# Modulation vectors on VectorE, GpSimd out of block 2's streams, a narrower product of the probabilities' remainder

## The chip, the cores and the metric

One core of a Trainium2 chip runs the whole program in one launch. The metric is the device time of that core in microseconds, from a launch with all inputs in the chip's memory to the output written; the number quoted is the median of several runs.

## The reference

Two transformer blocks, one after the other, of two layers each. The width is 1024; there are 256 latent tokens and 256 context tokens, and only the latent ones leave (so the second layer of each block computes no context output). Everything is float32.

```python
# block 1, layer l; the same for ctx with c_ctx while l == 0
m = split(silu(c) @ ada_w[l] + ada_b[l], 6)           # six modulation vectors of 1024
h = modulate(x, m[0], m[1])                           # x * (1 + scale) + shift
y = even_mixer(h, h_ctx) if l % 2 == 0 else odd_mixer(h, h_ctx)
x = layer_norm(alpha * x + m[2] * y)
x = layer_norm(alpha * x + m[5] * conv_ffn(modulate(x, m[3], m[4])))   # 1024 -> 2*2816 -> 1024
# block 2, layer l; the same for ctx while l == 0
m = split(silu(c) @ w_mod[l] + b_mod[l], 6)
h = rms_norm(x, g_pre_mix) * (1 + m[1]) + m[0]
y = token_mixer(h, hc)    # conformer conv + differential attention (8 heads) + multiscale pool, gated
x = x + m[2] * rms_norm(y, g_post_mix)
h = rms_norm(x, g_pre_ffn) * (1 + m[4]) + m[3]
x = x + m[5] * rms_norm(swiglu(h), g_post_ffn)                         # 1024 -> 2*2816 -> 1024
# differential attention, for each head
a = softmax(q1 k1) - lam * softmax(q2 k2);  o = a @ v
```

The six modulation vectors of a layer are a product of one row (latent) or two rows (latent and context) with a 1024 x 6144 matrix. There are four such matrices, one for each layer.

## The kernel before

**Products.** A float32 product is made of three products of rounded values: each operand is split into a rounded high part and a remainder, and `mm3` issues high x high, high x remainder and remainder x high. Weights come in 128-row pieces of up to 1024 columns: `wload` (L149) puts one into a tile `wr`, of which there are four, from the queue of SyncE; `wsplit` (L154) rounds it on ScalarE (`wh`, L159) and subtracts on VectorE or, if asked, on GpSimd (`wl`, L161). The tiles `wh` and `wl` have three buffers each.

**Order.** In the mixers (even, odd, and block 2's token mixer) the order is written out by hand: `main_stream` and a weaving function place lists of small steps (products of a group, attention units, extra items) one after the other. A `Stream` holds the weights of such a stage; splits from number `first` on go to GpSimd. In the FFNs the order of instructions on each engine is left to the framework's scheduler.

**Modulation vectors.** `ada` (L176) makes a list of items for a layer: eight chunks for each vector (128 rows of the matrix by 1024 columns), then a `bias` item (adds the bias, and for the two gates writes them to memory), and a `turn` item (transposes) for the others. A chunk runs in one of two ways. With no `acc_pool`, TensorE multiplies it: four unrounded matmuls, one for each quarter of the columns, on 32 of the array's columns each (L194). With `acc_pool` set (the large FFNs, of 512 tokens), VectorE multiplies the chunk by a column of silu(c) and adds it to a running sum (L201 for the first chunk, L204 for the others), once for the latent row and, where context is needed, once more; after the eighth chunk TensorE sums over the partitions with four matmuls for each of these rows (`pick`). A chunk occupies one `wr` tile until it is used.

Which items run where: the even mixer takes the rest of the first layer's vectors and as much of the second's as fits (eight items in each of five groups and 18 at the end, 58 in all); block 1's first FFN the remaining 38, on VectorE; the odd mixer 40 of block 2's first layer, in `extra` (14 and 22 at its end); block 1's second FFN (256 tokens, one item for each of its 22 pairs) the remaining 18, on TensorE; block 2's first FFN all 58 of block 2's second layer, on VectorE.

**A large FFN**: pairs of up-products j = 0 to 3 for each half of the tokens; pairs 4 to 10, with two items each; the first half of the down-product (two phases `nb`, six weight pieces each, one item after each piece); pairs 11 to 21, with two or three items each; the rest of the items; `mid()`, which prepares the next layer's factors; and the second half of the down-product.

**Block 2's attention** (`b2_attn`): for each head, the q, k, v products from a stream, rotary embedding (`rope`, L561, whose last addition is on GpSimd, L569), the stacking of q and k (L589), scores, softmax, the combination of the two probabilities on VectorE (L1516), transposes and the product with v. In that product the transposed probabilities H (rounded) and L (remainder) meet v, which lies as [high | remainder] in 256 columns; the result is later the sum of both halves of `oo`. Beside it the 31-tap convolution runs on VectorE (L1638).

**Gates of block 2's FFN.** `gg_bc` (L1315) loads the gain `g_post_ffn` into a tile `z`, the gate into `gbc`, and multiplies them on VectorE (L1322), at the FFN's start.

## Time and profile before

| | us |
|---|---|
| runs (three) | 2651.8, 2650.45, 2657.49 |
| median | 2651.8 |
| the profiled execution, as a run | 2655.9 |
| its span (first to last instruction) | 2654.1 |

The stages in the profiled span, by the lines that run: even mixer to 273, its output product and norm to 346, block 1's first FFN to 712, odd mixer to 842, its output to 895, block 1's second FFN to 1104, block 2's first attention stage to 1380, its branches and output product to 1703, its first FFN to 2082, the second attention stage to 2300, branches and output to 2456, and the last FFN to the end. The profile's page gives the busy time of each engine, PE being TensorE's matmuls, PEld its weight loads, DVE VectorE, ACT ScalarE, POOL GpSimd and SP SyncE; it also follows the chain of work that ended last. The granted clock is the clock that TensorE was given, as a share of full speed; its mean in this run is 0.983. A record's duration of a matmul is longer than its step, since matmuls overlap in the array: the distance from one start to the next is what a matmul takes in a sequence.

### The profile page before, as it was taken

What the parts mean: (1) busy time and instruction counts of PE and PEld (TensorE: products, weight loads), DVE (VectorE), ACT (ScalarE), POOL (GpSimd) and SP (SyncE); (2) the same over time, 40 slices, a digit from 0 to 9 for tenths busy, and PEclk for the clock granted to TensorE, in tenths of its full rate; (3) what the DMA queues carried; (4) which work ended last, traced back from release to release, by engine and by line L of the source; (5) the groups of instructions that cost most, each with busy time, mean ns of one, the idle gap of its engine ahead of it and who ended that gap; (6) DMA issues with size and microseconds to landing.
All of it is one profiled execution on the core that took longest, in us unless ns stands there. A gap on an engine that the chain in (4) does not pass through costs nothing.

```text
span 2654.1 us, 40807 instructions
## 1 busy us (share of the span) xinstructions
PE 2515.9 (95%) x15516; PEld 2183.4 (82%) x15516; DVE 1852.0 (70%) x3226; ACT 1230.0 (46%) x2329; POOL 407.9 (15%) x483
## 2 busy tenths in 40 slices
PE   7899899999998899999989999999999999898998
PEld 4787698788875799998877878888887999798997
DVE  5766797576877877556679755775457777887554
ACT  3554464144455555556652233532224565554543
POOL 4231100000121000243320000000000244200000
PEclk9999999999999899999999999999999999999999
DMA  8344766453556676531212234565656521356554
GB/s 270 112 153 162 265 213 194 157 166 108 178 178 218 197 232 188 175 88 54 66 53 88 88 96 150 177 199 177 192 163 195 158 80 61 95 161 208 171 182 147
DMA packets 129828, 412.37 MB, mean 155 GB/s; under 512 B 16640, under 2 KB 24992, under 8 KB 129632
## 3 DMA queue, kind: packets, MB, share of 16 engines
q1 hardware_dynamic: 119296, 386.45, 46.1%
q0 software_dynamic: 10048, 23.30, 2.9%
q8 instruction: 122, 2.00, 0.3%
q14 instruction: 74, 0.61, 0.1%
q10 hardware_dynamic: 288, 0.02, 0.0%
HBM read 408.59 MB, written 1.11 MB: 154 GB/s over the span
## 4 chain that ended last, share of the span: by engine, by line
PE 70%; DVE 13%; issue 6%; DMA 6%; ACT 4%; POOL 2%; SPq 0%; POOLq 0%; DVEq 0%; ACTq 0%
PE mm L168 62%; PE ax L168 3%; DVE wl L161 2%; DMA wr<-in_ada_w 2%; PE mm L194 1%; PE ax L600 1%; POOL rs_r L292 1%; DMA wr<-in_w_mod 1%; PE ax L611 1%; DVE ptl L615 1%; DMA gbc<-gd 1%; DMA s0w<-in_ada_w 1%; DVE cv L1638 1%; DVE p L1516 1%; ACT wh L159 1%
## 5 line engine op out<-in xcount | busy, mean ns | idle before, releaser
L159 ACT CAST wh<-wr 128x1024 fp32r<-128x1024 f32 (+2 forms) x580 | 572.4, 990 | 858.2 <-PE mm L168 669.1
L161 DVE TENSOR_TENSOR wl<-wr,wh 128x1024 fp32r<-128x1024 f32 (+2 forms) x494 | 570.5, 1158 | 273.1 <-ACT wh L159 270.4
L168 PE MATMUL mm<-hH,wh 128*128 128x256 f32 (+1 forms) x2176 | 708.5, 326 | 5.1 <-ACT wh L159 4.5
L168 PE MATMUL mm<-hH,wl 128*128 128x256 f32 (+1 forms) x2176 | 703.4, 324 | 3.5 <-DVE wl L161 3.3
L168 PE MATMUL mm<-hL,wh 128*128 128x256 f32 (+1 forms) x2176 | 703.2, 323 | 0.0
L168 PEld LDWEIGHTS mm<-hH,wh 128*128 128x128 f32 x2176 | 416.6, 192 | 46.6 <-issue 6.2
L168 PEld LDWEIGHTS mm<-hH,wl 128*128 128x128 f32 x2176 | 416.3, 191 | 37.0 <-DVE wl L161 5.3
L168 PEld LDWEIGHTS mm<-hL,wh 128*128 128x128 f32 x2176 | 416.6, 191 | 31.2
L168 PE MATMUL mm<-wh,hH 128*128 128x384 f32 (+1 forms) x864 | 278.2, 322 | 0.7 <-DVE hH L338 0.7
L168 PE MATMUL mm<-wl,hH 128*128 128x384 f32 (+1 forms) x864 | 270.4, 313 | 3.4 <-DVE wl L161 1.8
L168 PE MATMUL mm<-wh,hL 128*128 128x384 f32 (+1 forms) x864 | 269.7, 312 | 0.3 <-DVE hL L342 0.3
L161 POOL TENSOR_TENSOR wl<-wr,wh 128x768 fp32r<-128x768 f32 (+1 forms) x86 | 182.4, 2128 | 261.5 <-ACT wh L159 214.7
L168 PE MATMUL mm<-wh,gH 128*128 128x512 f32 x528 | 206.6, 392 | 3.4 <-DVE tm L1080 2.3
L168 PE MATMUL mm<-wl,gH 128*128 128x512 f32 x528 | 206.5, 391 | 2.8 <-DVE wl L161 2.8
L168 PE MATMUL mm<-wh,gL 128*128 128x512 f32 x528 | 206.0, 390 | 0.0
L168 PEld LDWEIGHTS mm<-wh,hH 128*128 128x128 f32 x864 | 164.9, 191 | 9.8 <-issue 6.9
L168 PEld LDWEIGHTS mm<-wl,hH 128*128 128x128 f32 x864 | 165.0, 191 | 6.9 <-DVE wl L161 2.7
L1638 DVE SCALAR_TENSOR_TENSOR cv<-u,cconv_w,cv 128x512 f32<-128x512 f32 (+1 forms) x240 | 168.4, 704 | 2.6
L168 PEld LDWEIGHTS mm<-wh,hL 128*128 128x128 f32 x864 | 164.7, 191 | 0.5 <-DVE hL L342 0.5
L204 DVE SCALAR_TENSOR_TENSOR adacc<-wr,cs,adacc 128x1024 f32<-128x1024 f32 x83 | 105.6, 1283 | 78.3 <-DMA wr<-in_w_mod 48.1
L292 POOL TENSOR_TENSOR rs_r<-rs_v,mhalf 128x1 f32<-128x1 f32 x44 | 41.6, 947 | 668.3 <-DVE rs_v L313 374.1
L168 PEld LDWEIGHTS mm<-wh,gH 128*128 128x128 f32 x528 | 99.4, 188 | 25.7 <-issue 4.8
(340 smaller groups left out, 4016.0 us busy)
## 6 DMA issues: line engine op xcount, KB each, us to landing
wr<-in_up SPq DMA_DIRECT2D x192, 512.0 KB, 3.8
wr<-in_dn SPq DMA_DIRECT2D x100, 512.0 KB, 3.8
wr<-in_w_mod SPq DMA_DIRECT2D x96, 512.0 KB, 4.4
wr<-in_ada_w SPq DMA_DIRECT2D x80, 512.0 KB, 4.6
wr<-in_wg SPq DMA_DIRECT2D x48, 512.0 KB, 3.5
wr<-in_glu SPq DMA_DIRECT2D x24, 512.0 KB, 3.8
wr<-in_qkv SPq DMA_DIRECT2D x32, 384.0 KB, 3.1
wr<-in_wo SPq DMA_DIRECT2D x24, 512.0 KB, 4.1
```

The costliest lines, as they stand in the source:

```text
L159: nc.scalar.copy(h[:, :n], w[:, :n])
L161: eng.tensor_tensor(l[:, :n], w[:, :n], h[:, :n], ALU.subtract)
L168: self.nc.tensor.matmul(o, s, m, start=start, stop=stop, skip_group_check=True)
L194: nc.tensor.matmul(st["pa"][32 * j:32 * j + 32, 0:256], a, x[:, j * 256:(j + 1) * 256], start=start, stop=stop, skip_group_check=True, til ...
L204: nc.vector.scalar_tensor_tensor(st["acc"][r], wt, cs[:, k, r:r + 1], st["acc"][r], ALU.mult, ALU.add)
L292: self.nc.gpsimd.tensor_tensor(o, i, self.mhalf[:, 0:n], ALU.pow)
L600: nc.tensor.transpose(pt[:, i * P:(i + 1) * P], s, self.idr)
L611: nc.tensor.transpose(pt[:, i * P:(i + 1) * P], s, self.idn)
L615: nc.vector.tensor_tensor(L, pt, H, ALU.subtract)
L1516: nc.vector.scalar_tensor_tensor(p0, p1, c[:, i:i + 1], p0, ALU.mult, ALU.add)
L1638: nc.vector.scalar_tensor_tensor(o, cb["u"][c][:, :, j:j + 256], cb["w"][:, c, j:j + 1], o, ALU.mult, ALU.add)
```

## The change

Three parts.

First, the items of `ada` are now kept by vector, and the vectors are dealt out anew. The even mixer gets vectors 2, 4 and 3 of its own layer alone (29 items: 5, 5, 5, 5, 4 in its groups and the rest at the end); block 1's first FFN gets vector 5 of that layer and 1, 0, 2, 4, 3 of the second layer (58 items, on VectorE); the odd mixer vectors 1, 0, 2 of block 2's first layer (29 items: 9 before its last group, the rest at the end); block 1's second FFN vector 5 of its own layer and 4, 3 of block 2's first (29 items, one for each of 14 pairs, then two); block 2's first FFN vector 5 of its own layer and all of the second's (67 items, on VectorE). Each chunk in a large FFN costs one or two units of credit, by its rows; each of the 30 places there adds 2.9 units, items run as long as the credit lasts, and a place stops after an item without a load. The gates' loads of block 1's FFNs are issued at the first use, `gg_bc` of block 2's FFNs in `mid()`.

Second, block 2's two streams no longer give splits to GpSimd, and its `rope` adds on VectorE. The powers of the norms stay on GpSimd, and so do the splits that the even and odd mixers give it.

Third, in block 2's product of probabilities and v, the remainder L is multiplied by v's high half only; L times v's remainder is left out.

```diff
-    def __init__(self, b, first=0, pool=None, n=0):
+    def __init__(self, b, first=None, pool=None, n=0):
...
-            self.hl[r] = self.b.wsplit(w, self.items[i][1], r >= self.first, own)
+            self.hl[r] = self.b.wsplit(w, self.items[i][1], self.first is not None and r >= self.first, own)
...
+    SHARE = 2.9
...
-                items.append((w[k * P:(k + 1) * P, m * D:(m + 1) * D], lambda wt, f=prod, k=k: f(wt, k=k)))
+                items.append((w[k * P:(k + 1) * P, m * D:(m + 1) * D], lambda wt, f=prod, k=k: f(wt, k=k),
+                              2 if parts.index(m) < ctx else 1))
                 if k == 1 and late is not None:
-                    items.append((None, late))
-            items.append((None, bias))
+                    items.append((None, late, 0))
+            items.append((None, bias, 0))
             late = None if m in (2, 5) else turn
-        if late is not None:
-            items.append((None, late))
-        return items
+            if m == 3:
+                items.append((None, late, 0))
+                late = None
+        return res
...
+    def share_ada(self, items, n):
+
+        self.credit += n
+        while items and items[0][2] <= self.credit:
+            self.credit -= items[0][2]
+            ap = items[0][0]
+            self.run_ada(items, 1)
+            if ap is None:
+                break
+        if not items:
+            self.credit = 0
...
-        nc.gpsimd.tensor_tensor(o, o, t2, ALU.add)
+        (eng or nc.gpsimd).tensor_tensor(o, o, t2, ALU.add)
...
-            gr["extra"] = self.stream_ada(ws, ada, (0, 8, 8, 8, 8, 8)[g])
+            gr["extra"] = self.stream_ada(ws, ada, (0, 5, 5, 5, 5, 4)[g])
...
-        last = self.stream_ada(ws, ada, 18)
+        last = self.stream_ada(ws, ada, 100)
...
-        extra = (0, 0, 4, 14, 22)
+        extra = (0, 0, 4, 9, 100)
...
                 for j in range(self.SKEW, 11):
                     up_pair(j, 0, 2)
-                    self.run_ada(ada, 2)
+                    self.share_ada(ada, self.SHARE)
                 for nb in range(2):
-                    banks = self.mmT(units(0, nb), gstat, range(4), 512, each=lambda: self.run_ada(ada, 1))
+                    banks = self.mmT(units(0, nb), gstat, range(4), 512, each=lambda: self.share_ada(ada, self.SHARE))
                     for t in range(4):
                         evac(t, nb, banks[t], 0)
                 for j in range(11, 22):
                     up_pair(j, 0, 2)
-                    self.run_ada(ada, 2 if j < 20 else 3)
+                    self.share_ada(ada, self.SHARE)
                 self.run_ada(ada, 100)
                 self.acc_pool = None
                 mid()
...
                 for j in range(NFF):
                     up_pair(j, 0, 1)
-                    self.run_ada(ada, 1)
+                    self.run_ada(ada, 1 if j < 14 else 2)
...
-            gts = {r: self.gate_bc(pool, key, 1, r, f"gbc{r}") for r in segs}
+            gts = {}
...
             def evac(t, nb, bank, kh):
+                if not gts:
+
+                    gts.update({r: self.gate_bc(pool, key, 1, r, f"gbc{r}") for r in segs})
...
-                            self.rope(pool, f, n64(b[:, 0:256]), rt("c", t, 4), rt("s", t, 4), 4)
+                            self.rope(pool, f, n64(b[:, 0:256]), rt("c", t, 4), rt("s", t, 4), 4, nc.vector)
...
                     self.mm(oo, H[:, c:c + P], vk, k == 0, False)
-                    self.mm(oo, L[:, c:c + P], vk, False, k == nk - 1)
+
+                    self.mm(oo[:, 0:P], L[:, c:c + P], vk[:, 0:P], False, k == nk - 1)
...
-            gg = self.gg_bc(pool, key, 1, segs, A["g_post_ffn"][l:l + 1])
+            gg = {}
...
             def mid():
+                gg.update(self.gg_bc(pool, key, 1, segs, A["g_post_ffn"][l:l + 1]))
...
-                    self.even_mixer(self.pool(s2, "att"), a0)
+                    self.even_mixer(self.pool(s2, "att"), a0[2] + a0[4] + a0[3])
...
-            self.b1_ffn(0, 512, a0, "b1l1")
+            self.b1_ffn(0, 512, a0[5] + a1[1] + a1[0] + a1[2] + a1[4] + a1[3], "b1l1")
...
-                    self.odd_mixer(self.pool(s2, "att1"), self.pool(s2, "att1u"), a2)
+                    self.odd_mixer(self.pool(s2, "att1"), self.pool(s2, "att1u"), a2[1] + a2[0] + a2[2])
...
-            ws = Stream(self, 10)
+            ws = Stream(self)
...
-            self.b1_ffn(1, 256, a2, None, early, late)
+            self.b1_ffn(1, 256, a1[5] + a2[4] + a2[3], None, early, late)
...
-            self.b2_ffn(0, 512, a3, False)
+            self.b2_ffn(0, 512, a2[5] + a3[1] + a3[0] + a3[2] + a3[4] + a3[3] + a3[5], False)
...
-            ws = Stream(self, 12)
+            ws = Stream(self)
```

## Rows read from the trace of the kernel before

**Rows 1.** The page: busy time by engine; shares of the last chain.
```profile
PE 2515.9 (95%) x15516; PEld 2183.4 (82%) x15516; DVE 1852.0 (70%) x3226; ACT 1230.0 (46%) x2329; POOL 407.9 (15%) x483
...
PE 70%; DVE 13%; issue 6%; DMA 6%; ACT 4%; POOL 2%; SPq 0%; POOLq 0%; DVEq 0%; ACTq 0%
```

**Rows 2.** Windows: stretch, length, busy PE, PEld, DVE, ACT, POOL, clock, DMA, GB/s.
```profile
65.00:273.00 208.00, 196.55 (x1452) 164.99 (x1451) 141.19 (x342) 109.79 (x301) 51.13 (x54) 0.99 0.46 149
457.00:521.00 64.00, 60.83 (x273) 49.18 (x272) 34.42 (x42) 14.57 (x17) 1.96 (x4) 1.00 0.49 158
712.00:842.00 130.00, 117.91 (x953) 90.15 (x952) 103.19 (x245) 66.93 (x158) 31.71 (x40) 0.95 0.56 177
1104.00:1380.00 276.00, 258.86 (x1705) 247.35 (x1703) 182.00 (x423) 163.96 (x442) 109.16 (x79) 0.99 0.25 75
...
2082.00:2300.00 218.00, 203.68 (x1633) 197.49 (x1632) 168.71 (x410) 130.37 (x318) 84.59 (x79) 0.98 0.27 82
...
895.00:1070.00 175.00, 174.69 (x1302) 160.25 (x1301) 132.92 (x209) 99.84 (x155) 5.21 (x10) 1.00 0.67 212
1800.00:1866.00 66.00, 66.00 (x305) 53.90 (x304) 34.78 (x38) 15.45 (x19) 1.96 (x4) 1.00 0.54 170
```

**Rows 3.** Timeline of PE around one chunk (start, duration, engine, line, operation).
```profile
196.18 0.28 PE L168 MATMUL mm<-ptl,v 128*128 128x256 f32 x1
196.39 0.64 PE L194 MATMUL mm<-wr,cs 128*32 128x256 f32 x8
...
197.24 0.34 PE L168 MATMUL mm<-wl,hH 128*128 128x384 f32 x1
```

**Rows 4.** Timeline of PE in block 2's product with v.
```profile
1256.71 0.28 PE L168 MATMUL ax<-v,pth 128*128 128x256 f32 x1
...
1256.83 0.28 PE L168 MATMUL ax<-v,ptl 128*128 128x256 f32 x1
```

**Rows 5.** Chain of waits at the odd mixer's end (start, duration, what).
```profile
817.33 5.47 DMA wr<-in_w_mod
...
826.52 7.88 DMA wr<-in_w_mod
```

**Rows 6.** Groups, whole span: xcount | busy us, mean ns | idle before.
```profile
L161 DVE TENSOR_TENSOR wl<-wr,wh 128x1024 fp32r<-128x1024 f32 x432 | 525.9, 1220 | 218.9 <-ACT wh L159 216.4
...
L204 DVE SCALAR_TENSOR_TENSOR adacc<-wr,cs,adacc 128x1024 f32<-128x1024 f32 x83 | 105.6, 1283 | 78.3 <-DMA wr<-in_w_mod 48.1 <-DMA wr<-in_ada_w 29.9
...
L194 PE MATMUL ax<-adacc,pick 128*32 128x256 f32 x88 | 6.6, 389 | 2.0 <-DVE adacc L204 2.0
```

**Rows 7.** Chain of waits at the start of block 2's first FFN.
```profile
1688.18 7.68 DMA z<-in_g_post_ffn
...
1695.96 1.22 DVE gbc L1322
```

**Rows 8.** POOL's subtractions in the first, then the second attention stage's window.
```profile
L161 POOL TENSOR_TENSOR wl<-wr,wh 128x768 fp32r<-128x768 f32 x32 | 60.7, 1907 | 80.9 <-ACT wh L159 78.4 <-PE mm L168 2.5
...
L161 POOL TENSOR_TENSOR wl<-wr,wh 128x1024 fp32r<-128x1024 f32 x24 | 58.8, 2452 | 75.9 <-ACT wh L159 63.1 <-issue 12.6
```

**Rows 9.** DVE: L1516 in the first, the second stage; L1638 there, over the span.
```profile
L1516 DVE SCALAR_TENSOR_TENSOR p<-p,cs,p 128x512 f32<-128x512 f32 x16 | 19.7, 1233 | 0.6
...
L1516 DVE SCALAR_TENSOR_TENSOR p<-p,cs,p 128x512 f32<-128x512 f32 x16 | 12.0, 752 | 0.6
...
L1638 DVE SCALAR_TENSOR_TENSOR cv<-u,cconv_w,cv 128x256 f32<-128x256 f32 x60 | 44.6, 743 | 0.4
...
L1638 DVE SCALAR_TENSOR_TENSOR cv<-u,cconv_w,cv 128x256 f32<-128x256 f32 x120 | 72.8, 612 | 0.7
```

**Rows 10.** Windows around two idle stretches of PE, columns as in rows 2.
```profile
1698.00:1704.00 6.00, 2.72 (x9) 2.13 (x10) 6.00 (x10) 3.46 (x6) 0.00 (x0) 0.66 0.07 6
...
2452.00:2458.00 6.00, 4.52 (x19) 3.77 (x19) 3.35 (x7) 2.33 (x6) 1.12 (x2) 0.50 0.58 188
2458.00:2464.00 6.00, 6.00 (x40) 5.99 (x40) 4.17 (x8) 2.04 (x4) 0.00 (x0) 0.74 0.07 29
```

More of the change, by code (lines that the diff above doesn't have):

```diff
@@ L188, in ada @@
         cs = self.cs[blk]
-        items, late = [], None
+        res, late = {}, None
         for m in parts:
-            st = {}
+            st, items = {}, []
+            res[m] = items
             def quarter(st, j, a, x, start, stop):
@@ L255, in run_ada @@
             if items:
-                ap, f = items.pop(0)
+                ap, f, _ = items.pop(0)
                 f(None if ap is None else self.wload(ap, D))
+    def share_ada(self, items, n):
[7 more added lines that the diff above has]
+        if not items:
+            self.credit = 0
     def stream_ada(self, ws, items, n):
@@ L263, in stream_ada @@
             if items:
-                ap, f = items.pop(0)
+                ap, f, _ = items.pop(0)
                 if ap is None:
@@ L558, in unit_slots, with rope @@
         return slots
-    def rope(self, pool, o, src, cosT, sinT, n):
+    def rope(self, pool, o, src, cosT, sinT, n, eng=None):
         nc = self.nc
@@ L1387, in e1 @@
                         if full:
-                            self.rope(pool, f, n64(b[:, 0:256]), rt("c", t, 4), rt("s", t, 4), 4)
+                            self.rope(pool, f, n64(b[:, 0:256]), rt("c", t, 4), rt("s", t, 4), 4, nc.vector)
                         else:
                             o = (h % 2) * P
-                            self.rope(pool, f[:, 0:2], n64(qs[t][:, o:o + P]), rt("c", t, 2), rt("s", t, 2), 2)
-                            self.rope(pool, f[:, 2:4], n64(b[:, 0:P]), rt("c", t, 2), rt("s", t, 2), 2)
+                            self.rope(pool, f[:, 0:2], n64(qs[t][:, o:o + P]), rt("c", t, 2), rt("s", t, 2), 2, nc.vector)
+                            self.rope(pool, f[:, 2:4], n64(b[:, 0:P]), rt("c", t, 2), rt("s", t, 2), 2, nc.vector)
                     else:
@@ L1655, in pool_items, with b2_mixer @@
         return [f for gi in range(4) for f in self.mmF_items(ws, self.A[f"wp{l}"][gi], lambda k: self.rhs(k, 0, T), T, done)]
-    def b2_mixer(self, l, T, cb, after, ws, pre, rate, ada=()):
+    def b2_mixer(self, l, T, cb, after, ws, pre, rate):
         nc, A = self.nc, self.A
@@ L1934, in build @@
             a3 = self.ada("b2l1", 2, A["w_mod"][1], A["b_mod"][1], ctx=2)
-            self.b2_mixer(0, 512, cb[0], lambda: after(0), ws, self.glu_items(ws, 0, cb[0], 0, 1), 1.0, a3)
-            self.b2_ffn(0, 512, a3, False)
+            self.b2_mixer(0, 512, cb[0], lambda: after(0), ws, self.glu_items(ws, 0, cb[0], 0, 1), 1.0)
+            self.b2_ffn(0, 512, a2[5] + a3[1] + a3[0] + a3[2] + a3[4] + a3[3] + a3[5], False)
             self.lst.close()
-            ws = Stream(self, 12)
+            ws = Stream(self)
             self.b2_mixer(1, 256, cb[1], lambda: after(1), ws, self.glu_items(ws, 1, cb[1], 0, 1), 0.6)
```

8 lines of the change are left out of this document (4 added, 4 removed).

## The prediction

> **What bounds the kernel now.** First the page's busy line and the chain of work that ended last [rows 1]: TensorE is busy for 95% of the span and 70% of that chain is TensorE; VectorE stands second with 70% busy and 13% of the chain, GpSimd has 15% and 2%. So work taken from TensorE counts nearly in full wherever TensorE is itself the limit, and VectorE is the engine to which this change adds. Next the same by stage, because the average hides where VectorE has room [rows 2]. TensorE is idle for 11.5 us of the 208 in the even mixer, 12.1 of 130 in the odd one, 0.3 of 175 in block 1's second FFN, 17.1 of 276 and 14.3 of 218 in the two attention stages of block 2. VectorE is at 79% in the odd mixer and 77% in the second attention stage, but only at 54% and 53% in the two stretches of the large FFNs where the product with the down weights runs. Last the rows of single instructions, for prices.
>
> **1. Modulation chunks leave the mixers.** One chunk (128 of the 1024 rows of one vector's weights) is eight records on TensorE. From the matmul before it to the second matmul after it the starts are 1.06 us apart [rows 3]; without it there would be one step of 256 columns, 0.12 [rows 4], and one of 384, 0.18 in proportion. So a chunk costs 0.76 us. The even mixer goes from 49 chunks to 24 (from 58 list items to 29): 25 x 0.76 = 19.0 us less. Against it stands what they cover: the list spread over its last units falls from 18 items to 5, and where TensorE would otherwise wait, a chunk was free. With no value left in those 11 or so chunks the gain is 19.0 - 8.4 = 10.6; with all of it, and half of the stage's idle time as waits for the chunks' own loads, it is 19.0 + 5.7 = 24.7. TensorE is 94% busy there, so I take a value nearer to the price, **-17** (-10 to -25).
>
> The odd mixer goes from 34 chunks to 24: 10 x 0.76 = 7.6. At its end the chain twice waits for a load of such a chunk, 5.5 and 7.9 us [rows 5]; with ten loads fewer the chunks are there earlier, but the waits end in the last units' own VectorE work (79% busy), which is late next. I take 5 of the 13.4 as gained and 3.5 as lost to tail steps that are no longer covered: **-9** (-3 to -15).
>
> **2. Chunks that stay on TensorE arrive in block 1's second FFN**: 14 become 24. TensorE has no idle time there, so 10 x 0.76 = 7.6, and 1.4 for a denser stream of loads at the end, where two items stand behind each pair: **+9** (+6 to +14).
>
> **3. Chunks accumulated by VectorE.** In block 1's first FFN the rows (one vector's chunk for one of latent and context) go from 31 to 72, in block 2's from 64 to 80. A row is 1.28 us of VectorE [rows 6]; TensorE pays only for the sum over partitions at a vector's end, eight records for each of latent and context: 6.6 / 11 = 0.60 us a set. There are five more sets in the first FFN (nine for four), two more in the second: +3 and +1.2. The new sharing gives 2.9 rows of credit at each of 30 places. Counting the credit through the lists, the twelve places within the down-product stretch (457 to 521 in block 1) come to 21 chunks and 35 rows, where 8 rows stand now: VectorE's 34.4 us grow by 27 x 1.28 = 34.6 to 69.0 in a stretch of 64. That is 5 too much. In block 2's stretch (1800 to 1866) 15 rows become 35: 34.8 + 25.7 = 60.5 of 66, which fits on average, though not in its second half, which has 19 of the rows and a burst of five chunks at its end. The later pairs get bursts of three to six chunks, ahead of subtractions that the next matmuls need. I charge 4 for bursts in block 1's FFN and 6 in block 2's with the second half's excess. At the end of block 2's FFN a tail of ten items is gone: about the 2.0 us for which TensorE waits for an accumulation [rows 6]. Together **+12** for block 1's first FFN (0 to +30) and **+6** for block 2's (-3 to +25). The gates are now loaded at the first use rather than at the start of block 1's FFNs; GpSimd's queue, which issues them, has next to nothing else there (1.96 us busy in 64), so the load is issued long before and costs nothing; were it issued only at its place, VectorE would stand for up to 7.7 us, as for the gain in [rows 7].
>
> **4. GpSimd leaves block 2's streams.** 66 remainder subtractions (32 of 768 columns and 10 of 1024 in the first layer, 24 of 1024 in the second) and 48 rope additions move to VectorE. GpSimd takes 1.9 and 2.5 us for one subtraction and has long idle time before each [rows 8]; VectorE takes 1.22 for 1024 columns [rows 6], so between 0.92 and 1.22 for 768 (I take 0.96). First layer: 32 x 0.96 + 10 x 1.22 + 16 additions of 256 columns at 0.48 (the small convolution step of [rows 9], freed of its stretch) = 50.6. Second: 24 x 1.22 + 32 additions of 128 columns at an estimated 0.3 = 38.9. But VectorE's two-input operations stretch beside GpSimd's: the probability combination means 1.23 us in the first layer and 0.75 in the second, 16 x 0.48 = 7.7 us; the convolution step of 256 columns means 0.74 us in the window of the second attention stage and 0.61 over all 120, so 0.48 for the 60 outside it, 60 x 0.26 = 15.7 [rows 9]. These two kinds alone give back 7.7 and 15.7. VectorE would stand at 182 + 43 = 225 of 276 and 169 + 23 = 192 of 218: full, not over. What TensorE gains is bounded by its idle time, 17.1 and 14.3; what it may lose is a weight product that waits for a subtraction now queued on VectorE behind the convolution. A step is quicker by 1.2 us once it starts (2.45 against 1.22). I take rather less than half of the idle time: **-8** (-14 to +8) and **-6** (-14 to +10).
>
> **5. Narrower product of the remainder.** 160 matmuls go from 256 moving columns to 128. The steps are 0.12 us [rows 4]. If the time falls in proportion this gives 160 x 0.06 = 9.6; if a step is bound by something else, nothing. **-4** (-9.6 to +19, see the second rival).
>
> **6. Gate and gain product moved.** At the start of block 2's first FFN the chain waits 7.7 us for a load of the gain, and VectorE then multiplies twice for 1.2 us while the last normalised rows wait behind it [rows 7]; TensorE is busy for 2.7 of the 6 us after 1698 and at a granted clock of 0.66 [rows 10]. That is 3.3 lost, 0.9 by the clock, and about 2 in the last FFN, where the same product stands in the same place. In the middle of the FFN the load is hidden by some 30 us of down product (half of the stretch of 64). **-6** (-9 to -2).
>
> **Sum**: -17 - 9 + 9 + 12 - 8 - 6 - 4 - 6 + 6 = -23 us. The profiled run took 2655.9, so 2632.9; the median of the runs is 4.1 below the profiled one: **2629 us**.
>
> **Rivals.** First, **VectorE becomes the bound of the large FFNs**, and the kernel is slower. Four weight buffers rotate between down weights and chunks, and a chunk's buffer is held until VectorE has added both its rows, 2.57 us; a subtraction behind it is late by as much. It decides once VectorE's demand exceeds the stretch, as 69.0 of 64 does. If all twelve down loads of block 1's stretch and half of block 2's meet such a chunk, TensorE loses 18 x 2.57 = 46, of which 10 are in the sum: 2665. For it: the 69.0. Against it: 54% now, and that the chunks' sums have no hurry.
>
> Second, **the narrow rounded product isn't cheaper, but dearer**: no row shows a rounded product of under 256 columns. If it ran like the unrounded ones, the chunk of [rows 3] gives the price: 0.64 for 256 columns less the 0.16 by which a record outlasts its step [rows 4], halved, is 0.24, so +0.12 x 160 = +19 in place of -4: 2652, no change. Nothing in the profile speaks for or against it.
>
> Third, **the clock falls where the fillers were**. After an idle time the granted clock is 0.50, the 1.2 GHz level, for 6 us and 0.74 for the next 6 [rows 10]: TensorE, busy for 4.5 and 6.0 of them, loses 2.3 + 1.6 = 3.8. If the mixers' ends, with fewer chunks, fall into it twice, the time is 2637. The Trainium skill's page "TensorE: Matmul & The Clock Gate", section "HAM oscillation — how this bites in real kernels", says that waits between groups of matmuls make the clock fall again and again, which speaks against taking fillers out of a stage that waits. The traces agree that an idle stretch is followed by the low level (0.50).
>
> That the change doesn't do what it says (chunks left over and run in one go after the pairs) I give nothing: by the count of credit both lists end before the last pairs.
>
> **How the numbers follow.** Forecast 0.57, first rival 0.15, second 0.18, third 0.10. What a measurement of this kernel can tell from no change is about 0.3%, 8 us: faster is below 2644, slower above 2660. The forecast's own range, 2605 to 2650 from the bounds above (they won't all fall on one side), lies mostly below 2644 (0.50 of 0.57); the third rival adds 0.08, the second and first 0.06: 0.64 faster. The second gives most of "same", with 0.07 of the forecast: 0.20. The first gives most of "slower": 0.16. To hold 8 in 10 the range takes in the second rival and the first up to its price: 2600 to 2666.
>
> **What would show it.** Windows at the same stages: the even and odd mixers shorter by 17 and 9, block 1's second FFN longer by 9 and its first by 12, VectorE near 90% or more in the down-product stretches with TensorE waiting for the subtraction's line if the first rival holds; the convolution step at 0.48 in the second layer; the step of the narrow product in the timeline under 0.12 (or near 0.24); no wait for the gain at block 2's first FFN. The forecast is wrong if a large FFN grows by over 30 us, or if an attention stage gets longer because its products wait for VectorE.

## The result and the profile after

The changed kernel takes 2667.7 us (median of five runs, 2665.4 to 2669.8) against 2651.8 before: a ratio of 1.0055, 95% interval 1.0038 to 1.0071. It is slower by 16 us; 2629 was forecast, with 2600 to 2666 as the range.

The page of the profiled execution (span 2665.8), busy time by engine, answers to [rows 1]:

```profile
PE 2513.3 (94%) x15372; PEld 2184.4 (82%) x15372; DVE 1938.5 (73%) x3397; ACT 1228.1 (46%) x2329; POOL 237.1 (9%) x369
```

TensorE has 144 records fewer and is busy for 2.6 us less, so over the span the added time is idle time; in single stages a part of it is busy time at a lower clock, as the attention stage below shows. To see where it lies, both traces are cut at the same instructions: the first matmul of each stage. First the kernel before (stretch, length, busy PE, PEld, DVE, ACT and POOL, granted clock, DMA share, GB/s): even mixer; block 1's first FFN, its first down product and the pairs behind it; odd mixer and its output; the pairs of the second FFN; first attention stage; the pairs of block 2's first FFN up to its down product, and that product; second attention stage.

```profile
0.00:282.20 282.20, 249.35 (x1807) 198.50 (x1807) 181.30 (x429) 135.92 (x354) 86.39 (x124) 0.99 0.56 182
...
461.50:526.10 64.60, 61.43 (x275) 49.66 (x274) 33.67 (x43) 14.02 (x16) 1.96 (x4) 1.00 0.51 164
526.10:647.60 121.50, 121.50 (x547) 99.45 (x546) 83.53 (x104) 48.69 (x63) 3.10 (x6) 1.00 0.43 132
711.60:845.70 134.10, 121.09 (x981) 92.11 (x980) 105.88 (x249) 69.30 (x162) 33.81 (x45) 0.95 0.57 182
845.70:885.90 40.20, 29.75 (x130) 21.48 (x130) 30.99 (x48) 16.27 (x28) 8.37 (x21) 0.85 0.72 252
885.90:1024.90 139.00, 138.69 (x1173) 131.95 (x1171) 111.32 (x187) 84.20 (x138) 6.14 (x11) 0.99 0.66 214
...
1136.70:1400.50 263.80, 246.28 (x1530) 231.01 (x1529) 188.49 (x437) 153.34 (x435) 92.92 (x76) 0.99 0.20 61
1679.70:1813.30 133.60, 128.90 (x755) 113.67 (x754) 95.32 (x113) 51.70 (x78) 7.00 (x10) 0.97 0.58 188
1813.30:1874.70 61.40, 61.40 (x284) 50.09 (x283) 26.92 (x27) 15.81 (x20) 1.96 (x4) 1.00 0.55 175
2094.00:2297.60 203.60, 189.28 (x1515) 183.17 (x1514) 156.43 (x384) 117.83 (x299) 82.05 (x75) 0.97 0.25 77
```

The same stretches of the changed kernel, same columns:

```profile
0.00:270.40 270.40, 235.61 (x1604) 196.99 (x1604) 177.83 (x423) 136.10 (x355) 79.48 (x110) 0.98 0.47 146
...
447.30:520.10 72.80, 63.88 (x301) 50.26 (x299) 60.39 (x68) 12.65 (x14) 3.96 (x8) 1.00 0.70 225
520.10:649.00 128.90, 127.02 (x556) 102.02 (x557) 95.44 (x121) 50.08 (x64) 5.13 (x10) 0.96 0.55 173
713.00:843.40 130.40, 113.89 (x902) 88.46 (x900) 108.24 (x251) 71.48 (x164) 30.20 (x37) 0.97 0.51 156
843.40:877.00 33.60, 26.43 (x114) 20.66 (x114) 27.32 (x42) 13.88 (x24) 8.65 (x23) 0.87 0.65 207
877.00:1031.00 154.00, 149.86 (x1268) 136.14 (x1267) 112.44 (x190) 86.65 (x140) 10.32 (x18) 0.98 0.73 239
...
1145.50:1415.40 269.90, 249.32 (x1531) 231.93 (x1530) 203.85 (x489) 150.91 (x435) 14.93 (x26) 0.97 0.20 60
1694.60:1821.20 126.60, 125.54 (x753) 111.18 (x752) 85.21 (x102) 51.48 (x78) 6.93 (x12) 1.00 0.56 176
1821.20:1888.60 67.40, 63.39 (x302) 50.33 (x301) 52.28 (x54) 15.94 (x20) 3.95 (x8) 1.00 0.73 242
2105.70:2307.50 201.80, 189.02 (x1515) 183.32 (x1513) 160.63 (x440) 115.92 (x299) 8.22 (x20) 0.97 0.26 78
```

Read line by line: the even mixer is 11.8 us shorter (its output another 2.6), the odd mixer with its output 10.3, block 2's first pairs 7.0. Longer are block 1's first FFN by 8.2 and 7.4, its second by 15.0, the first attention stage by 6.1 and the steps ahead of it by 2.8 (54.6 us for 51.8), block 2's first down product by 6.0. The second attention stage gives 1.8. All stages together give the 11.7 us between the two profiled spans; by the medians it is 16, since the profiled execution of the kernel before was 4 us above its median. One caution: stages whose instructions are the same in two kernels differ by up to some 4 us between profiles (the odd mixer takes 130.5 us in a run below in which only block 2 was changed, 134.1 here), so a stage's difference counts where several runs show it. Over all profiles below, the odd mixer itself takes 130.5 to 134.1 us with the old dealing of vectors and 129.9 to 132.8 with the new one, so hardly less; its output takes 39.5 to 41.9 and 33.6 to 33.7. What is sure of the 10.3 is the 7 us in the output.

Three places show what the lost time is. First, the end of the first down product in block 1's first FFN (the timeline of TensorE, then that of ScalarE):

```profile
516.15 0.39 PE L171 MATMUL mm<-wh,gL 128*128 128x512 f32 x1
520.13 0.72 PE L171 MATMUL mm<-hH,wh 128*128 128x512 f32 x1 [3.60 <-ACT wh L162]
...
524.35 0.79 PE L171 MATMUL mm<-hH,wl 128*128 128x512 f32 x1 [1.75 <-DVE wl L164]
...
519.04 1.05 ACT L162 CAST wh<-wr 128x1024 fp32r<-128x1024 f32 x1 [11.31 <-DMA wr<-in_up]
```

And the windows around it:

```profile
513.00:520.00 7.00, 3.54 (x17) 2.56 (x15) 5.71 (x8) 0.96 (x1) 0.00 (x0) 1.00 0.97 344
520.00:524.00 4.00, 2.37 (x4) 0.93 (x4) 4.00 (x7) 1.13 (x2) 0.00 (x0) 0.53 0.62 222
524.00:530.00 6.00, 5.65 (x13) 4.46 (x14) 4.45 (x6) 1.05 (x1) 0.00 (x0) 0.50 0.66 203
```

The sharing puts five chunks behind the last weight piece of this product. The queue of SyncE shows them (its issues, then the largest group of its waits from 503.5 to 516.5 us: total, times, longest):

```profile
504.08 8.23 SPq L154 DMA_DIRECT2D wr<-in_ada_w  x5
513.78 2.15 SPq L154 DMA_DIRECT2D wr<-in_up  x2
...
SPq L154 <- DVE adacc L208: 3.4, 3, 1.4
```

The next weights (`in_up`) are issued 9.7 us after the first of the five chunks, because the issues stand in one order and those ahead wait, 3.4 us of it for additions on VectorE, which give tiles back. The DMA engines are then at 0.97 and 344 GB/s, ScalarE waits 11.3 us for the next weights and TensorE 3.6 us; then it runs at a granted clock of about 0.5, the 1.2 GHz level, for ten microseconds, with a second wait of 1.8 us in them.

Second, the middle of the same product (VectorE's timeline, then TensorE's): four chunk rows and, just before them, the taking over of four finished sums (L1098, L1101) stand ahead of one subtraction.

```profile
485.07 4.86 DVE L208 SCALAR_TENSOR_TENSOR adacc<-wr,cs,adacc 128x1024 f32<-128x1024 f32 x4
489.86 1.22 DVE L164 TENSOR_TENSOR wl<-wr,wh 128x1024 fp32r<-128x1024 f32 x1
...
491.13 0.50 PE L171 MATMUL mm<-wl,gH 128*128 128x512 f32 x1 [3.43 <-DVE wl L164]
```

Third, the first attention stage: two subtractions, now on VectorE, stand ahead of the stacking of k for which TensorE waits (VectorE, then TensorE).

```profile
1187.00 1.81 DVE L164 TENSOR_TENSOR wl<-wr,wh 128x768 fp32r<-128x768 f32 x2
...
1189.13 0.41 DVE L610 TENSOR_TENSOR kst<-mm,kst 128x256 fp32r<-128x256 f32 x1
...
1189.69 0.41 PE L171 MATMUL mm<-wh,hH 128*128 128x384 f32 x1 [1.79 <-DVE kst L610]
```

### The profile page after: what moved, and what is told of

Read it like the earlier page. It is cut to its first block, busy times and chain, and to the rows that moved or that the text cites. A ratio compares the mean times of both kernels' runs of the same rounds, so it can differ in the third digit from the quotient of the medians.

```text
span 2665.8 us, 40496 instructions
## 1 busy us (share of the span) xinstructions
PE 2513.3 (94%) x15372; PEld 2184.4 (82%) x15372; DVE 1938.5 (73%) x3397; ACT 1228.1 (46%) x2329; POOL 237.1 (9%) x369
## 4 chain that ended last, share of the span: by engine, by line
PE 36%; DVE 10%; ACT 4%; issue 4%; POOL 1%; DMA 1%; DVEq 0%; POOLq 0%; ACTq 0%
PE mm L171 34%; DVE wl L164 2%; ACT wh L162 1%; DVE cv L1660 1%; DVE pnm L1492 1%; ACT p L1517 1%; PE ax L171 1%; POOL rs_r L310 1%; DVE ptl L633 1%; DVE kst L610 0%; PE ax L618 0%; DVE x L1329 0%; DVE adacc L208 0%; ACT p L1524 0%; DVE p L1537 0%
## 5 line engine op out<-in xcount | busy, mean ns | idle before, releaser
L164 DVE TENSOR_TENSOR wl<-wr,wh 128x1024 fp32r<-128x1024 f32 (+2 forms) x560 | 642.8, 1150 | 358.1 <-ACT wh L162 355.7
L171 PEld LDWEIGHTS mm<-hH,wl 128*128 128x128 f32 x2176 | 418.0, 192 | 46.0 <-DVE wl L164 13.7
L208 DVE SCALAR_TENSOR_TENSOR adacc<-wr,cs,adacc 128x1024 f32<-128x1024 f32 x133 | 167.4, 1278 | 34.5 <-DMA wr<-in_w_mod 29.6
L1660 DVE SCALAR_TENSOR_TENSOR cv<-u,cconv_w,cv 128x512 f32<-128x512 f32 (+1 forms) x240 | 146.5, 613 | 2.5
L171 PEld LDWEIGHTS mm<-wl,gH 128*128 128x128 f32 x528 | 99.1, 188 | 28.3 <-DVE wl L164 8.1
L171 PEld LDWEIGHTS mm<-wh,gL 128*128 128x128 f32 x528 | 99.1, 188 | 20.4
```

The costliest lines, as they stand in the source:

```text
L164: eng.tensor_tensor(l[:, :n], w[:, :n], h[:, :n], ALU.subtract)
L171: self.nc.tensor.matmul(o, s, m, start=start, stop=stop, skip_group_check=True)
L208: nc.vector.scalar_tensor_tensor(st["acc"][r], wt, cs[:, k, r:r + 1], st["acc"][r], ALU.mult, ALU.add)
L1660: nc.vector.scalar_tensor_tensor(o, cb["u"][c][:, :, j:j + 256], cb["w"][:, c, j:j + 1], o, ALU.mult, ALU.add)
```

## The experiments

Each ran beside the kernel before on the same chip; the ratios are to that kernel's runs, with 95% intervals.

| run | what it is | ratio | interval |
|---|---|---|---|
| only_vec | before + part 2 | 1.0029 | 1.0017 to 1.0041 |
| only_splits | before + subtractions of part 2 | 0.9992 | 0.9979 to 1.0004 |
| only_rope | before + additions of part 2 | 1.0004 | 0.9988 to 1.0020 |
| only_mod | the change without parts 2 and 3 | 1.0052 | 1.0036 to 1.0068 |
| only_gain | before + gain's product in the middle | 0.9982 | 0.9969 to 0.9996 |
| only_narrow | before + part 3 | 1.0008 | 0.9998 to 1.0018 |
| spread | change, second FFN's pairs of chunks spread | 1.0077 | 1.0055 to 1.0098 |
| one_row | change, one row a chunk in block 1's first FFN | 1.0053 | 1.0038 to 1.0068 |
| cap2 | change, at most two chunks a place | 1.0043 | 1.0026 to 1.0061 |
| mixed | parts of both, see below | 1.0018 | 1.0008 to 1.0028 |
| few_taps | before, 2 of 31 taps | 0.9918 | 0.9900 to 0.9937 |
| few_taps_vec | the same + part 2 | 0.9906 | 0.9889 to 0.9923 |
| even_spread | redistribution without crowded places | 0.9941 | 0.9919 to 0.9963 |
| one_load | change, second chunk of a pair not loaded | 1.0026 | 1.0013 to 1.0039 |

**Which part.** Four runs took the change apart.

```diff
# only_vec: rope(..., nc.vector) and
-            ws = Stream(self, 10)
+            ws = Stream(self, 1000)
-            ws = Stream(self, 12)
+            ws = Stream(self, 1000)
```

> The kernel before with GpSimd's part alone changed: no splits of block 2's streams on GpSimd, rope's addition on VectorE. Theory A (from the two traces: the first attention stage with what leads to it is 8 us longer, the branches about 4, the second stage 3 shorter; VectorE works in order and a subtraction stands ahead of steps for which TensorE waits): 2657 to 2663, that is 5 to 11 us slower than before, with the first attention stage 6 to 10 us longer. Rival (the loss there comes from another part, and the part by itself does what was forecast): 2637 to 2650, with both stages shorter.

> The kernel before with the 66 subtractions of block 2's streams on VectorE, rope's addition left on GpSimd. Theory A (the subtractions of 1 to 1.2 us each delay what stands behind them in VectorE's order): most of the loss of the whole part, 3 to 9 us slower than before. Rival (rope's addition on VectorE is what costs): within 3 us of before or faster.

> The kernel before with rope's 48 additions alone on VectorE, the subtractions left on GpSimd. Theory A: within 3 us of before, rather faster, since a step of 0.3 to 0.4 us replaces one of 0.5 to 0.7 and a handover in both directions. Rival (the additions on VectorE are what costs): 4 us or more slower.

```diff
# only_mod: the change with Stream(self, 10), Stream(self, 12), rope on GpSimd, and
-                    self.mm(oo[:, 0:P], L[:, c:c + P], vk[:, 0:P], False, k == nk - 1)
+                    self.mm(oo, L[:, c:c + P], vk, False, k == nk - 1)
```

> The change with GpSimd's part and the narrow product undone: the modulation vectors dealt out anew, together with the gain's product in the middle of the FFN, which the new order of vectors needs. Theory A (by stages of the two traces: even mixer and its output 15 us shorter, block 1's first FFN 16 longer, odd mixer and its output 10 shorter, block 1's second FFN 15 longer, block 2's first FFN 3 shorter with 7 of it from the gain): 3 us slower than before, between 2651 and 2658. Rival (the loss of the whole change lies here): 2662 to 2670.

Part 2 alone costs 0.3%, theory A. But neither half of it does so alone: the subtractions by themselves are within 0.1% of before and so are the additions, so the expectation that the subtractions alone make the kernel slower fell. In the stage they do carry most: in the profiles the first attention stage (263.8 before) is 268.1 with the subtractions, 264.0 with the additions and 271.4 with both. With the subtractions alone the second attention stage, with the steps ahead of it, is 4.8 us shorter (225.4 for 230.2), which makes up for the first. The redistribution alone costs 0.5%, which is the rival's result, not the 3 us that the two traces' stages added up to: its own profile shows the same stages as the change's (first FFN +9.6 and +6.6, second FFN +15.0, block 2's first pairs -7.0), and the sum over all its stages is 8 us; the medians, 12 us apart, say more, since its profiled execution was 1.4 us below its median and that of the kernel before 4 us above.

**Why part 2 costs in the first stage.** The convolution's taps were cut to see whether VectorE's queue is the reason. Both kernels leave 29 of the 31 taps out.

```diff
-                nc.vector.scalar_tensor_tensor(o, cb["u"][c][:, :, j:j + 256], ...)
+                if j < 2:
+                    nc.vector.scalar_tensor_tensor(o, cb["u"][c][:, :, j:j + 256], ...)
```

> The kernel before with 2 of the 31 taps of block 2's convolution (the other 29 left out): the reference for the next run. Theory A: VectorE isn't the bound of the attention stages, so they shorten by less than 8 us each; the branches too, where left taps run.

> The same 2 taps, with GpSimd's part changed as well. Theory A (the subtractions and additions stand in VectorE's order among other work, above all the convolution's steps, and are late through that): against the run with few taps the first attention stage is no more than 2 us longer, for 7.5 with all taps. Rival (VectorE is a longer way for these steps in itself, since the handovers from ScalarE and back lie in one order): 5 to 8 us longer, as with all taps.

The windows of the first attention stage, with few taps, without and with part 2 (one line of each kernel):

```profile
1132.20:1395.00 262.80, 246.23 (x1531) 231.20 (x1530) 154.44 (x395) 153.55 (x435) 89.60 (x76) 0.99 0.21 62
```

```profile
1131.30:1394.80 263.50, 248.53 (x1531) 231.93 (x1530) 174.53 (x445) 151.67 (x435) 13.62 (x26) 0.98 0.21 62
```

With VectorE at 59% and then 66% of the stage part 2 costs 0.7 us; with all taps, at 71% and then 75%, it costs 7.6. So theory A: the moved steps are late, and make others late, through what else stands in VectorE's order. It is not a matter of a full engine: 75% is busy. The waits of TensorE say which: those for `r1s` (4.1 us) and `kst` (1.4 to 2.0) come with part 2 whether the taps are there or not, and in their place the wait for `ptl` falls from 8.3 to 1.5; what the taps add is the wait for the norm of the heads (`os`), 4.3 to 7.5 us with all taps and 3.5 to 3.4 with few. Of the 7.6 us only 2.2 are idle time of TensorE; the other 5.4 are longer busy time, at a granted clock of 0.97 for 0.99. Over the whole kernel part 2 with few taps is 3 us faster, not clear of noise. The expectation for few_taps held in the first stage (1.0 us shorter) and failed in the second (11.6). In the second attention stage, where part 2 gains with all taps (203.6 before, 198.3 in only_vec), it costs 2.0 with few (192.0, 194.0); much of that stage's gain goes with its clock, 0.97 before and 1.00 in only_vec, and the change itself has 201.8 at 0.97.

**The narrow product and the gain.**

```diff
# only_gain
-            gg = self.gg_bc(pool, key, 1, segs, A["g_post_ffn"][l:l + 1])
+            gg = {}
...
             def mid():
+                gg.update(self.gg_bc(pool, key, 1, segs, A["g_post_ffn"][l:l + 1]))
```

> The kernel before with the product of gate and gain in the middle of block 2's FFNs, nothing else. Theory A (the changed kernel's first FFN of block 2 is 7 us shorter in its first pairs and 2 in its last products; the redistribution alone then costs about 20): 2642 to 2648, 6 to 10 us faster than before. Rival (that stage became shorter because of the modulation items): within 3 us of before.

> The kernel before with the remainder's product on 128 columns, nothing else. Theory A (in the changed kernel a narrow step takes 0.06 us but the wide one before it 0.17 in place of 0.12, so a pair takes 0.23 for 0.24): 0.5 to 3 us faster than before, that is 2650 to 2653. Rival (the steps shorten in proportion): 9 us faster. Third (the second attention stage is hurt by it, which was 3 us longer in the changed kernel than with GpSimd's part alone): slower by 2 or more.

The gain's product in the middle, alone, gains 0.2%: between the two expectations, 3 of the first 133.6 us where the change gains 7. The trace tells why (VectorE, first in only_gain, then in the changed kernel):

```profile
1694.44 1.23 DVE L1322 TENSOR_TENSOR gbc<-gbc,z 128x1024 f32<-128x1024 f32 x1 [4.17 <-DMA z<-in_g_post_ffn]
```

```profile
1841.53 2.35 DVE L1343 TENSOR_TENSOR gbc<-gbc,z 128x1024 f32<-128x1024 f32 x2
```

Although it is written behind all of the FFN's pairs, the scheduler of the FFN puts the product at the FFN's start, where its inputs are there. In the changed kernel the gate is vector 5, which that FFN itself computes, and so the product can't come early. The run mixed, further down, has the product written in the middle too, but its gate from an earlier stage; there it is early again, and the first pairs take 130.7 us as in only_gain:

```profile
1702.62 1.23 DVE L1345 TENSOR_TENSOR gbc<-gbc,z 128x1024 f32<-128x1024 f32 x1 [5.26 <-DMA z<-in_g_post_ffn]
```

So 3 of the 7 us come with the new line alone, and the other 4 only with the vector's place. In the last FFN, whose gate is known, the product stays early and nothing is gained (196.8 us before, 196.9 in only_gain, from its first product to the end).

The narrow product gives nothing that can be measured. Its steps (TensorE, changed kernel) answer to [rows 4]:

```profile
1267.12 0.22 PE L171 MATMUL ax<-v,ptl 128*128 128x128 f32 x1
1267.18 0.33 PE L171 MATMUL ax<-v,pth 128*128 128x256 f32 x1
1267.35 0.22 PE L171 MATMUL ax<-v,ptl 128*128 128x128 f32 x1
```

A narrow matmul takes 0.06 us, half of before, but the wide one that follows now takes 0.17 in place of 0.12: 0.23 for a pair that took 0.24.

**What costs in the large FFNs.** Two runs on the changed kernel: one halves VectorE's rows at the same loads (leaving out the context's row in block 1's modulation), the other caps a place at two chunks.

```diff
# one_row
-            def prod(wt, m=m, k=0, st=st, rows=2 if parts.index(m) < ctx else 1):
+            def prod(wt, m=m, k=0, st=st, rows=2 if parts.index(m) < ctx and key[:2] == "b2" else 1):
# cap2, in share_ada
-        while items and items[0][2] <= self.credit:
+        loads = 0
+        while items and items[0][2] <= self.credit and loads < 2:
...
+            loads += ap is not None
```

> The change with VectorE adding only the latent row of block 1's modulation chunks in its first FFN (the context's row is left out, its vectors then hold the bias alone): 48 rows in place of 72, with the same loads at the same places. Theory A (VectorE's rows stand ahead of the subtractions and hold the weight buffers): that FFN is 8 to 16 us shorter than in the change, back at 0 to 8 above before, total 2652 to 2660. Rival (the 17 further loads and the sums on TensorE are what costs): at most 4 us shorter, total 2663 to 2668.

> The change with at most two chunks at each place of the large FFNs, whatever credit is left; the rest comes later. Theory B (what costs in those FFNs is the burst of five loads at the end of the first down products: the weights' loads queue behind it, TensorE stands idle for 3.8 and 2.1 us and then runs at the low clock for some 10 us): block 1's first FFN 7 to 11 us shorter than in the change, block 2's 3 to 5, total 2652 to 2658. Rival (the number of chunks as such, 48 for 31, costs): at most 4 us shorter in all, 2663 or more.

The first down product's window in the two (one_row, then cap2) against 72.8 us in the change:

```profile
446.90:519.90 73.00, 64.52 (x286) 50.63 (x284) 43.29 (x52) 12.53 (x14) 3.98 (x8) 0.98 0.67 219
```

```profile
447.40:512.50 65.10, 63.23 (x299) 50.05 (x297) 54.75 (x61) 13.17 (x15) 4.08 (x8) 1.00 0.69 218
```

With 17 us less of VectorE's time the stretch is as long as in the change, so VectorE's load as a whole is not what is paid. This run has a limit: the five chunks of the burst have one row each in the change already, so it leaves the burst as it is (TensorE waits 3.7 us behind it). The waits behind VectorE in the middle did shrink, from 4.9 to 1.7 us, and one of 3.1 at the stretch's start took their place. With at most two chunks a place the stretch is back within 1 us of the 64.6 of the kernel before, and the pairs behind it (128.9 in the change) take 122.6. Theory B holds for these stretches; its total (2652 to 2658) was missed. cap2 as a whole is still slow, at 2664.6 us, since the cap leaves items over, which run in one go after the last pair: six chunks in block 1's FFN (1.9 us), but 14 in block 2's, whose later pairs take 136.2 us for 125.6. In mixed 14 are left in block 1's FFN:

```diff
# mixed: the change with cap2, without part 3 and without part 2 in block 2's first layer and rope, and
-        extra = (0, 0, 4, 9, 100)
+        extra = (0, 0, 4, 14, 22)
-                    self.run_ada(ada, 1 if j < 14 else 2)
+                    self.run_ada(ada, 1)
# a1[5] to block 1's first FFN, a2[4], a2[3], a2[5] to the odd mixer and the second FFN
```

> The even mixer and the large FFNs as in the change, with the cap of two chunks, and the whole second layer of block 1 in the first FFN; the odd mixer and block 1's second FFN with their items as before; the gain's product moved; streams of block 2's first layer and rope as before, those of its second layer on VectorE; the wide product. By the stages of the runs so far: even mixer -15, first FFN +7 to +10, gain -5 to -9, second attention stage -3 to -5: 2630 to 2642, faster than both. Rival (the stages don't add, or eight more chunks in the first FFN bring its waits back): 2645 or more.

mixed takes 2657.5 us, not 2630 to 2642. The rival's second half came true: the remainder stops TensorE for 13.7 us (waits of TensorE at the end of those pairs).

```profile
PE ax L198 <- DVE adacc L208: 13.7, 1, 13.7
```

**What costs in block 1's second FFN.** The chunks were spread, then the second load of a place was left out.

```diff
# spread
-                    self.run_ada(ada, 1 if j < 14 else 2)
+                    self.run_ada(ada, 2 if j % 3 == 2 else 1)
# one_load: j >= 14 runs one item with its load, and one more on the tile that is there
+                    if j >= 14 and ada:
+                        ap, f, _ = ada.pop(0)
+                        f(None if ap is None else self.last_w)
```

> The change with the items of block 1's second FFN spread evenly: two behind every third pair, one behind the others, in place of one behind each of 14 and two behind each of the last eight. Same chunks, same engine. Theory A (of the 15 us there, 7.5 are the twelve further chunks and the rest waits for the load and the split where two chunks follow each other): 3 to 7 us faster than the change, 2661 to 2665. Rival (a chunk simply costs 1.2 us there): as the change, 2666 to 2669.

> The change with the second chunk behind each of the last eight pairs of block 1's second FFN computed from the tile that is already there (its own load is left out, so those vectors are sums over a wrong chunk). TensorE's instructions are the same, six to eight loads fewer. Theory C (in a pair's 6.5 us there is room for three loads, not four: two weights and one chunk): that FFN is 4 to 8 us shorter than in the change. Rival (the second chunk's time on TensorE, its sums and the clock): within 2 us of the change.

Spreading gains nothing (156.5 us for 154.0, where kernels with the same items there take 152.8 to 156.3): two chunks behind a pair cost as much wherever they stand. Without the second load the same matmuls take 146.7 us and TensorE has no idle time at all:

```profile
876.80:1023.50 146.70, 146.70 (x1267) 134.45 (x1267) 112.92 (x190) 84.90 (x140) 10.23 (x18) 1.00 0.71 234
```

So theory C: 7.7 of the 15 us are the twelve further chunks (146.7 less 139.0, 0.64 a chunk), the rest is the fourth load in the time of a pair. Whether it is the four `wr` tiles or the DMA engines that have no room for it is open, since no run has another number of tiles. In the last 56 us of the stretch SyncE's queue waits for 14.6 us on matmuls of chunks, which hold a tile, and for 2.4 in one_load.

**A version without crowded places.**

```diff
# even_spread: the change without parts 2 and 3; SHARE 3.2, the cap of two, no stop after an item without a load;
-        extra = (0, 0, 4, 9, 100)
+        extra = (0, 0, 4, 12, 20)
-                    self.run_ada(ada, 1 if j < 14 else 2)
+                    self.run_ada(ada, 1)
# vectors 1, 0, 2 of block 2's first layer, 5 of block 1's second, then 4, 3: 36 items in the odd mixer, 22 in the second FFN
```

> The redistribution with no place that gets more than two chunks in a large FFN (no stop after an item without a load, credit of 3.2 a place, two chunks left over in block 2's FFN), one item behind each pair in block 1's second FFN and seven more in the odd mixer; the gain's product moved; GpSimd's part and the product of the remainder as before. Theory B (only crowded places cost; chunks of a large FFN in places of one or two are nearly free): even mixer and output -14, first FFN 0 to +4, odd mixer, its output and second FFN -2 to +3, block 2's first FFN -2 to -6: 2635 to 2645, faster than before by 8 to 16. Rival (the number of chunks in a large FFN costs wherever they stand): 2650 or more.

It takes 2639.5 us, 0.6% less than the kernel before (ratio 0.9941) where the change takes 0.55% more, so it is faster than both, as theory B has it. Its windows for the even mixer, the first FFN's down product and the pairs behind it, the second FFN's pairs, and block 2's first pairs and down product:

```profile
0.00:269.30 269.30, 234.31 (x1605) 194.37 (x1605) 177.81 (x424) 136.08 (x355) 79.67 (x110) 0.99 0.46 146
...
446.30:513.80 67.50, 64.44 (x309) 50.29 (x308) 57.89 (x66) 13.62 (x15) 3.98 (x8) 1.00 0.71 231
513.80:635.70 121.90, 121.88 (x548) 99.70 (x549) 93.41 (x118) 48.76 (x64) 5.13 (x10) 1.00 0.54 172
...
867.50:1010.20 142.70, 142.64 (x1204) 133.20 (x1203) 112.91 (x189) 85.54 (x141) 6.25 (x11) 0.99 0.68 228
...
1670.20:1796.90 126.70, 125.64 (x753) 111.23 (x753) 89.36 (x105) 51.40 (x78) 6.93 (x12) 1.00 0.59 190
1796.90:1862.00 65.10, 63.98 (x310) 50.48 (x308) 50.96 (x53) 15.08 (x19) 3.96 (x8) 1.00 0.73 242
```

The same 48 chunks as in the change cost the first FFN's two stretches 3.3 us in place of 15.6, and VectorE is busy for 86% of the down product's stretch, in which TensorE is idle for 3.1 us.

## Why the prediction was wrong

The measured time lies 39 us above the forecast. The step that failed is above all step 4, which priced GpSimd's part at -14 by a share of TensorE's idle time: alone it costs 6 to 8 us, some 21 of the 39. Next is the term of 1.4 us for the loads in step 2, which came as 7.3, with 2.8 more behind that FFN; then step 5, with nothing measurable for -4. Measured alone, part 1 with the gain is 12 to 14 us slower than before, where -5 was forecast (-17 - 9 + 9 + 12 - 6 + 6). The parts alone add up to 18 to 24 us, somewhat more than the 16 of the whole.

- **Step 1, chunks out of the mixers: the size was right, the odd mixer's reason was not.** -17 and -9 were forecast, -14.4 and -10.3 came. In the even mixer 19.0 by price less 14.4 leaves about 5 us of cover, and 8.4 was set as its most. In the odd mixer the chunks had filled idle time: the mixer itself is hardly shorter over all profiles, for the 7.6 forecast, and the gain of about 7 us is at its output, where the forecast had 5 gained by earlier loads and 3.5 lost again.
- **Step 2, block 1's second FFN: a term was mis-sized.** TensorE's 7.6 was 7.7, in part by luck: the window has twelve further chunks at 0.64 and not ten at 0.76, since two of the old list's 14 ran before it, in the odd mixer's output. The 1.4 "for a denser stream of loads" was 7.3, and 2.8 more came in the steps behind that FFN (54.3 to 54.6 us in every kernel with the new items there, 51.3 to 52.3 in the others; why was not tested). The text counted a chunk by TensorE's time and left out that every chunk is a 512 KB load in a stretch that already had three of them.
- **Step 3, the large FFNs: the sums near, the cause wrong.** +15.6 came for +12, and in block 2's +6.0 and -2.1 for +6. But VectorE's demand of 69.0 in 64 us, on which the step and the first rival rest, isn't what was paid: 60.4 us were done in 72.8, and taking 17 of them away (one_row) left the stretch at 73.0. The step saw bursts of three to six chunks and priced them at 4 us by VectorE's order; each is also up to five loads ahead of the weights, with idle time and low clock after it. How much of the 3.4 us behind four rows in the middle is VectorE's order alone is open. The first rival's time, 2665, is 3 us from the result by luck: its mechanism, VectorE as the bound, is not what the runs show, and GpSimd's part is in the result too.
- **Step 4, GpSimd out of block 2: the sign was wrong in the first layer.** The stretch of VectorE's operations did vanish: the combination (L1516 there, L1537 here) means 0.752 us in both stages now for 1.23 [rows 9], and VectorE's busy time grew by 15 us in the first stage and 9 in the steps ahead of it, not by 43, and in the second stage by 4, not by 23. But the argument went from "full, not over" to a share of TensorE's idle time. What counts in that stage is how late a step is on VectorE, as few_taps_vec shows; TensorE's waits for the norm of the heads went up, and those for the remainder of the probabilities (`ptl`) down (first the kernel before, then the changed one, waits within the stage: total, times, longest).

```profile
PE ax L600 <- DVE ptl L615: 8.3, 6, 1.9
PE ax L1564 <- DVE os L1559: 4.3, 8, 1.5
```

```profile
PE ax L1586 <- DVE os L1581: 8.4, 9, 2.8
PE mm L171 <- DVE r1s L1531: 4.1, 5, 0.8
...
PE ax L618 <- DVE ptl L633: 1.5, 1, 1.5
```

  Of the 6.1 us by which the stage is longer, 3.1 are idle time of TensorE and 3.0 longer busy time at a clock of 0.97 for 0.99; a loss by the clock was no term of this step. The gain forecast for the second layer was 6; 1.8 came here, and 1.8 to 5.3 in the kernels with part 2 (201.8 to 198.3 us for 203.6).
- **Step 5, the narrow product: mis-sized.** By its steps it is worth 1.6 us (160 x 0.01) in place of 4, and nothing was measured, because the next wide step takes what the narrow one saves. The second rival, a dearer narrow product, is refuted: 0.06 us.
- **Step 6, the gain: the size was right (-7.0 in the first pairs for -6), the reason in part wrong.** The product's new line alone gave 3 us; what keeps the product from the start of the FFN is that its gate isn't known yet. The 2 us of the last FFN did not come.
- **The third rival** came in another place than it was put: the clock fell further not at the mixers' ends (0.87 in the odd mixer's output, 0.85 before) but after the burst in the first FFN, to 0.50 to 0.53 for ten microseconds, after a wait of 3.6 us. The page named there, the Trainium skill's "TensorE: Matmul & The Clock Gate", tells in its section "HAM oscillation — how this bites in real kernels" of matmuls that wait for loads again and again and start at the low clock each time. The trace agrees for one such wait: 3.6 us, then 0.53.

The range missed by 2 us. The bounds of the single steps would have allowed for more (+14 in step 2, +8 in step 4's first layer), but they were narrowed because "they won't all fall on one side"; steps 2, 4 and 5 fell on the same side.

## What to carry to other kernels

Work that fills gaps must be dealt out by every resource that it takes, here a load and a buffer as well as an engine's time, and evenly: the same 48 chunks cost 15.6 us with a burst of five and 3.3 with at most two a place. An engine at 75% that works in order is not free for a step on which another engine waits; moving such a step there is priced by what stands ahead of it, not by its share of busy time. Where a scheduler orders the work, as in these FFNs, an instruction can run as soon as its data are ready, so moving its line alone may move nothing.

## What the runs showed of the hardware

A rounded matmul of 128 moving columns takes a step of 0.06 us, and the 256-column one behind it 0.17 where it takes 0.12 behind another wide one; alternating the two saves 0.01 us a pair. VectorE's combination of two 128x512 tiles took 1.23 us on average in the first attention stage with GpSimd's subtractions and additions beside it, 0.89 with the additions alone (only_splits) and 0.75 with neither (only_vec); a one-column operation (L1513) took 0.55, 0.22 and 0.22. The time that this gave back did not shorten the stage. In the first FFN five chunk loads stood ahead of a weight's load in SyncE's queue, and it was issued 9.7 us after the first of them.
